# Two more pairs of gate columns through the seven-product blocks, and a new share of filler between them and the attention stages

## The chip, the cores and the metric

The kernel runs on one core of a Trainium2 chip. The metric is the device time of one launch, in microseconds (us); lower is better. Engines are called as in the profile: PE (TensorE's matmuls), PEld (its weight loads), DVE (VectorE), ACT (ScalarE), POOL (GpSimd) and SP (SyncE, which issues nearly all DMAs here).

## The reference

One layer of an encoder on 1024 tokens of width 1024, in float32. One input projection is cut into ten parts, two attentions use them, and gates mix their outputs:

```python
h = rmsnorm(x, attn_norm_g)
proj = h @ w_in
(c_q, c_kv, k_rope, z_mla, q_dil, k_dil, v_dil, z_dil,
 g_mla, g_dil) = jnp.split(proj, split_points, axis=-1)
a_out = mla_attention(c_q, c_kv, k_rope, positions, mla_q_norm_g, mla_kv_norm_g, w_uq, w_ukv)
y_mla = (a_out * jax.nn.silu(z_mla)) @ w_o_mla
d_out = dilated_mixture(q_dil, k_dil, v_dil, positions)
y_dil = (d_out * jax.nn.silu(z_dil)) @ w_o_dil
gate_mla = jax.nn.sigmoid(g_mla + b_gate[:D_MODEL])
gate_dil = jax.nn.sigmoid(g_dil + b_gate[D_MODEL:])
merged = gate_mla * y_mla + gate_dil * y_dil
return x + merged @ w_out
```

The dilated mixture has three groups of eight heads, with windows and dilations (128, 1), (512, 4), (2048, 16); their outputs are combined by softmax denominators. The latent attention has eight heads and is dense. A last RMSNorm follows. The gates' 2048 columns of `w_in` are what the change moves about.

## The kernel before, in words

**Precision.** Every float32 operand is split into a high and a low part (`split`, L148: a cast on ACT, L150, and a subtraction on POOL or DVE, L151), and a product is three matmuls (`mm3`, L142 to L146). A *column tile* is 128 columns of `w_in`; there are 48 of them in the array `wt`.

**Stages.** First come the projections (to 226.9 us in the profile): latents, rotary tables, the token factors `rcol` (one over the RMS of each token, by column) and `R` (the same as a row over all partitions), the up-projections of the latent attention, and the values of the dilated heads (`dil_v`, L422). There the order of instructions is left to a scheduler. From the block stage on the order is that of the code.

`token_factors` (L268) squares and sums the tokens, takes the inverse root on DVE (`rsqrt`, L198), copies it to `rcol` (L277), transposes it on PE (L279), copies the row (L281), and sends it through DRAM to `R`. `latents` (L338) scales the latents on DVE by `rcol` and by their own factors (L349 to L357) and transposes them on PE (L364). `dil_v` makes eight tiles of 128 tokens for each of six quarters; a tile `dv_st` takes the high part on ACT (L445), the low part on DVE (L446), and is stored by SP. There are three buffers of it.

**Block stage** (`blocks`, L649; 226.9 to 531.7 us). An item is two column tiles against all tokens, a 2 x 2 by 2 x 2 block product made with seven products in place of eight. Each is four `mm3` of 512 tokens (`block_product`, L507): 84 matmuls for an item, where plain column tiles take 96. POOL makes the differences of weight blocks (`block_minus`, L495) and splits (`block_operand`) five products ahead (`LEAD`). DVE and ACT add the products and finish: rotary embedding for twelve items of queries and keys, and for gate items the factor `R` and a tanh (the sigmoid by half angles), stored to `s_gt`. The rotary tables `cs_d` are multiplied by `R` ahead of it, in four operations on POOL (L1635). `BLOCK_GATES` (L50) names the first tile of each gate item: four items, eight of the sixteen gate tiles.

**Dilated stage** (`attention`, L1316; 531.7 to 829.7 us). The heads go in four pairs. A pair has two heads each of the groups 0 and 1, four units a head, and two units of group 2 ("class units"): 18 units a pair, 72 in all. A *tick* t works on several units at once, in this order (L1332 to L1352):

```python
do(t, 3)        # transposes: PE, then a cast on ACT (L1152)
do(t + 2, 0)    # scores: PE (L1120, L1121)
do(t, 4)        # low part: DVE (L1156)
do(t + 2, 1)    # masked maxima: DVE (L1130)
self.feed(DIL_FEED[g])
do(t - 2, 6)    # copy of half a result: ACT (L1180), every other tick
do(t + 2, 2)    # exponentials: ACT (L1137)
do(t - 2, 7)    # sum of a result: DVE (L1194), every other tick
self.feed(DIL_FEED[g])
do(t - 1, 5)    # values: PE (L1168, L1175)
```

Class units have their own lines (scores L1231, exponential L1242, transposes L1248, cast L1250, values L1262). When a unit is the last of a head, the load of the queries and keys of the head after the next is issued (`at_r<-s_dq`, `at_r<-s_dk`). The combine of a pair (`combine`, L1371) runs under the next pair's ticks: statistics through DRAM, exponents, quotients, factors through DRAM (`s_rr`), and products on POOL and DVE (L1450, sums L1454).

**Filler.** `feed(n)` (L66) adds n to a debt and issues that many steps of `gate_fill` (L718). This makes plain column tiles, `ZG` (L49): the eight tiles of z and the other eight gate tiles. A tile has 16 steps, a step one `mm3` of 512 tokens. Around its matmuls a tile needs a weight load of 512 KB, two casts on ACT and two subtractions on POOL, and for each half a product with `R` on DVE (L728), a tanh on ACT (L730 for z, L734 for gates), for z two operations on POOL (L731, L732), and a store. `DIL_FEED` (L32) has the steps of each of the two feeds in a tick: by group 0, 1, 2, and 3 for the ticks behind the last unit. Nine steps go ahead of the first tick. What is left is spread over the first 29 ticks of the latent attention (829.7 to about 1146 us), behind which come the output projections.

Of the kernel before, what the change touches and what calls it, by code (L numbers as in the profile page):

```python
# [10 lines left out]
F32 = mybir.dt.float32  # L11
# [19 lines left out]
FIRST_FEED = 9  # L31
DIL_FEED = (1.33, 1.33, 2.3, 1.8)  # L32

# [14 lines left out]

ZG = (4, 5, 6, 7, 0, 1, 2, 3, *range(16, 24))  # L49
BLOCK_GATES = (8, 10, 12, 14)  # L50

# [9 lines left out]
class Net:  # L61
# [205 lines left out]

    def token_factors(self, xp, pp):  # L268

        nc, a = self.nc, self.a  # L270
        ss = xp.tile([128, 8], F32, name="x_ss", bufs=1)
        for t in range(8):
            x = xp.tile([128, D], F32, name="x_in")
            self.dma(x, a["x"][128 * t:128 * t + 128, :])
            nc.scalar.activation(out=x, in_=x, func=AF.Square, accum_out=ss[:, t:t + 1])
        y = self.rsqrt(ss, 1.0 / D, xp, 8)
        nc.vector.tensor_copy(self.rcol, y)  # L277
        pt = pp.tile([128, 512], F32, name="pj")
        nc.tensor.transpose(pt[:8, :128], y, self.ident)  # L279
        row = xp.tile([8, 128], F32, name="x_row", bufs=1)  # L280
        nc.vector.tensor_copy(row, pt[:8, :128])  # L281
        self.dma(self.rs, row)
        flat = self.rs.rearrange("a b -> (a b)")
        self.dma(self.R, flat.partition_broadcast(128))
# [137 lines left out]
    def dil_v(self, g, quad, tp, pj):  # L422
# [12 lines left out]
        for t in range(8):  # L435
# [7 lines left out]
            if g < 2:  # L443
                st = tp.tile([128, 4, 2, 64], F32R, name="dv_st")
                nc.scalar.mul(st[:, :, 0], pv, f)  # L445
                nc.vector.scalar_tensor_tensor(out=st[:, :, 1], in0=pv, scalar=f, in1=st[:, :, 0].bitcast(F32), op0=ALU.mult, op1=ALU.subtract)  # L446
                x = slice(quad * 512, quad * 512 + 512)
                if g == 0:
                    dst = self.dv[0][128 * t + 64:128 * t + 192, x]
                else:  # L450

                    dst = self.dv[1].rearrange("(r m) x -> m r x", r=4)[32 * t:32 * t + 32, :, x]
                self.dma(dst, st.rearrange("p h a d -> p (h a d)"))
            else:
                st = tp.tile([128, 4, 64], F32, name="dv_s2")
                nc.scalar.mul(st, pv, f)
                self.dma(self.dv[2][2 * quad:2 * quad + 2, 128 * t:128 * t + 128].rearrange("a t x -> t a x"), st.rearrange("p (a h) d -> p a (h d)", h=2))
# [191 lines left out]
    def blocks(self, items, tp, pp):  # L649
# [14 lines left out]
        with self.tc.manual_schedule():  # L664
            for x in range(1, places + 14):
# [15 lines left out]
                self.block_minus(j + LEAD + 1, items)  # L681

                if x == places - 1:
                    self.close_sums()
                    self.open_areas(0)
                    for load in self.items[0][:2]:
                        load()
# [883 lines left out]
    def run(self):  # L1571
        tc, nc = self.tc, self.nc
        with ExitStack() as ctx:
# [28 lines left out]
            with tc.tile_pool(name="wpx", reuse_waits="tile", bufs=2, side="right") as self.wpx, tc.tile_pool(name="cosd", reuse_waits="tile", bufs=1, side="right") as dpool, ExitStack() as sums:  # L1602
                with tc.tile_pool(name="pj_a", reuse_waits="tile", bufs=NB_A, space=PSUM) as pj, tc.tile_pool(name="dvp", reuse_waits="tile", bufs=3, side="right") as vp:
                    with tc.tile_pool(name="lp", reuse_waits="tile", bufs=1) as lp, tc.tile_pool(name="pj_l", reuse_waits="tile", bufs=8 - NB_A, space=PSUM) as pl:
                        with tc.tile_pool(name="wl", reuse_waits="tile", bufs=1) as wl, tc.tile_pool(name="xp", reuse_waits="tile", bufs=3) as xp:
                            self.latent_proj(lp, wl, xp, pj)
                            self.tables(xp)
                            self.token_factors(xp, pl)
                            m = cp.tile([128, 896], F32, name="masks")
# [17 lines left out]
                    with tc.tile_pool(name="bs", reuse_waits="tile", bufs=1) as tp:  # L1627
                        self.block_sums(sp, tp)
                        self.dil_v(1, 0, vp, pj)
                    for g, quad in ((1, 1), (2, 0), (2, 1)):  # L1630
                        self.dil_v(g, quad, vp, pj)
                    for x in (self.cos_d, self.sin_d):
                        for half in range(2):
                            c = slice(512 * half, 512 * half + 512)
                            nc.gpsimd.tensor_tensor(out=x[:, c], in0=x[:, c], in1=self.R[:, c], op=ALU.mult)  # L1635
                    for r in (0, S + 64):
# [106 lines left out]
```

## Time and profile before

| | |
|---|---|
| three runs | 1252.14, 1256.76, 1256.94 us; median 1256.76 |
| the profiled execution | 1254.46 us |
| its span | 1252.5 us, mean granted clock of PE 0.99 |
| PE busy | 1212.4 us (97%), 6909 matmuls |
| PEld, DVE, ACT, POOL busy | 1064.5, 730.8, 622.0, 570.2 us |
| DMA | 221.37 MB, 177 GB/s in the mean |

The profile is of one execution. A line of the timeline has the start from the beginning of the span, the length, the engine, the line of the kernel, the operation, its output and inputs with their shapes; in brackets stands how long the engine was idle just before, and who ended that. A line of groups has, behind the bar, the busy time, the mean length in ns, and the idle time before these instructions. A matmul is listed with its whole latency, so matmuls overlap and the distance of their starts tells the pace. A wait costs time only on the engine that the rest waits for.

### The profile page before, as it was taken

To read this page: it belongs to the slowest core of one execution; us is meant where nothing else is said; L and a number is where in the kernel's file an instruction comes from. 1 tells how busy PE (TensorE), PEld (TensorE's weight loads), DVE (VectorE), ACT (ScalarE), POOL (GpSimd) and SP (SyncE) were. 2 spreads that over 40 slices of the span, in tenths; PEclk is the share of its full clock that TensorE was granted. 3 is DMA by queue.
4 is the path that set the end of the run, shared out by engine and by line. 5 is a ranking of instruction groups with operands and counts; after the bars stand their busy time and mean duration, and the time that the engine had idled before them with its cause. 6 is when DMAs were issued, how large, how long until landed. Compare 5 with 4: busy or idle time off the path is not lost.

```text
span 1252.5 us, 19486 instructions
## 1 busy us (share of the span) xinstructions
PE 1212.4 (97%) x6909; PEld 1064.5 (85%) x6909; DVE 730.8 (58%) x1304; ACT 622.0 (50%) x1300; POOL 570.2 (46%) x482
## 2 busy tenths in 40 slices
PE   8979999999999999999999999999999999999998
PEld 8979999888888888888888889878878888888886
DVE  7473534467657653345555575647766767759542
ACT  6534345444343344455554666545655656654232
POOL 2352218877777777543464442415521201168322
PEclk9989999999999999999999999899999999999999
DMA  9847589365445642496887898964634445225241
GB/s 333 225 157 283 196 302 317 103 180 156 135 132 165 174 127 100 122 268 197 233 257 200 207 294 212 266 175 116 178 128 119 110 118 135 85 96 182 84 151 51
DMA packets 126416, 221.37 MB, mean 177 GB/s; under 512 B 28072, under 2 KB 60400, under 8 KB 121392
## 3 DMA queue, kind: packets, MB, share of 16 engines
q1 hardware_dynamic: 126320, 220.14, 59.5%
q8 instruction: 54, 0.88, 0.3%
q14 instruction: 42, 0.34, 0.1%
HBM read 149.24 MB, written 70.85 MB: 176 GB/s over the span
## 4 chain that ended last, share of the span: by engine, by line
PE 75%; DMA 11%; DVE 4%; ACT 4%; issue 3%; POOL 1%; SPq 1%; ACTq 0%; POOLq 0%; DVEq 0%
PE bank L145 5%; PE bank L144 5%; PE bank L146 5%; PE pj L145 4%; PE bank L871 4%; PE pj L144 4%; PE pj L146 4%; DMA at_r<-s_dk 3%; PE st_a L144 2%; PE st_a L145 2%; PE st_d L145 2%; PE st_c L145 2%; PE st_d L146 2%; PE st_a L146 2%; PE st_c L146 2%
## 5 line engine op out<-in xcount | busy, mean ns | idle before, releaser
L151 POOL TENSOR_TENSOR w_l<-w_raw,w_h 128x512 fp32r<-128x512 f32 x188 | 247.5, 1330 | 276.7 <-ACT w_h L150 218.1
L150 ACT CAST w_h<-w_raw 128x512 fp32r<-128x512 f32 x188 | 112.6, 621 | 110.1 <-POOL w_raw L495 92.7
L144 PE MATMUL bank<-at_r,w_h 128*128 128x512 f32 x344 | 142.8, 415 | 0.0
L879 DVE TENSOR_TENSOR at_r<-bank,at_r 128x512 fp32r<-128x512 f32 x128 | 88.0, 688 | 84.5 <-ACT at_r L873 84.2
L145 PE MATMUL bank<-at_r,w_h 128*128 128x512 f32 x344 | 136.6, 397 | 0.6 <-POOL at_r L151 0.6
L146 PE MATMUL bank<-at_r,w_l 128*128 128x512 f32 x344 | 136.7, 397 | 0.0
L873 ACT CAST at_r<-bank 128x512 fp32r<-128x512 f32 x128 | 74.9, 586 | 72.5 <-PE bank L871 71.9
L145 PE MATMUL pj<-w_l,at_r 128*128 128x256 f32 x384 | 109.7, 286 | 0.0
L146 PE MATMUL pj<-w_h,at_r 128*128 128x256 f32 x384 | 109.6, 285 | 0.0
L144 PE MATMUL pj<-w_h,at_r 128*128 128x256 f32 x384 | 109.5, 285 | 0.0
L1137 ACT ACTIVATE at_f<-at_f,at_f 128x256 f32<-128x256 f32 x128 | 64.1, 502 | 52.1 <-DVE at_f L1130 51.8
L1156 DVE TENSOR_TENSOR at_r<-bank,at_r 128x512 fp32r<-128x512 f32 x64 | 43.9, 686 | 70.4 <-ACT at_r L1152 70.3
L495 POOL TENSOR_TENSOR w_raw<-w_raw 128x512 f32<-128x512 f32 x64 | 82.8, 1294 | 0.1
L871 PE MATMUL bank<-consts,at_f 128*128 128x128 f32 x512 | 77.2, 273 | 1.7 <-ACT at_f L863 1.1
L146 PEld LDWEIGHTS bank<-at_r,w_l 128*128 128x128 f32 x344 | 65.7, 191 | 14.9
L146 PEld LDWEIGHTS pj<-w_h,at_r 128*128 128x128 f32 x384 | 74.2, 193 | 1.0
L145 PEld LDWEIGHTS pj<-w_l,at_r 128*128 128x128 f32 x384 | 74.3, 193 | 0.7
L144 PEld LDWEIGHTS pj<-w_h,at_r 128*128 128x128 f32 x384 | 74.2, 193 | 0.7
L145 PEld LDWEIGHTS bank<-at_r,w_h 128*128 128x128 f32 x344 | 65.9, 192 | 9.9 <-POOL at_r L151 1.0
L144 PEld LDWEIGHTS bank<-at_r,w_h 128*128 128x128 f32 x344 | 65.8, 191 | 9.2
L895 PE MATMUL bank<-at_r,at_r 128*128 128x256 f32 x256 | 67.7, 285 | 1.3 <-ACT at_r L873 1.3
L896 PE MATMUL bank<-at_r,at_r 128*128 128x256 f32 x256 | 67.5, 285 | 0.9 <-DVE at_r L879 0.9
(321 smaller groups left out, 3325.3 us busy)
## 6 DMA issues: line engine op xcount, KB each, us to landing
w_raw<-wt SPq DMA_DIRECT2D x48, 512.0 KB, 3.7
at_r<-s_dq SPq DMA_DIRECT2D x32, 512.0 KB, 7.3
s_dk<-dq_st SPq DMA_DIRECT2D x80, 128.0 KB, 2.4
s_dv<-dv_st SPq DMA_DIRECT2D x32, 256.0 KB, 3.0
s_dq<-dq_st SPq DMA_DIRECT2D x64, 128.0 KB, 2.4
zt<-s_gt SPq DMA_DIRECT2D x32, 256.0 KB, 4.5
w_raw<-wv SPq DMA_DIRECT2D x12, 512.0 KB, 5.8
at_r<-s_dk SPq DMA_DIRECT2D x8, 576.0 KB, 11.3
```

The source lines that it names most:

```text
L144: mm(out, lh, rh, start=start, stop=False, skip_group_check=skip)
L145: mm(out, lh, rl, start=False, stop=False, skip_group_check=skip)
L146: return mm(out, ll, rh, start=False, stop=stop, skip_group_check=skip)
L150: self.nc.scalar.copy(out=h, in_=raw)
L151: sub.tensor_tensor(out=l, in0=raw, in1=h.bitcast(F32), op=ALU.subtract)
L495: self.nc.gpsimd.tensor_tensor(out=b[out], in0=b[x], in1=b[y], op=ALU.subtract)
L871: self.nc.tensor.transpose(pt[:, o:o + 128], self.P[k, b][:, 128 * kc:128 * kc + 128], self.ident)
L873: self.nc.scalar.copy(out=h, in_=pt)
L879: self.nc.vector.tensor_tensor(out=l, in0=pt, in1=h.bitcast(F32), op=ALU.subtract)
L895: mm(out, vv[:, kc], ph[:, x], start=kc == 0, stop=False)
L896: mm(out, vv[:, kc], pl[:, x], start=False, stop=kc == 7)
L1137: nc.scalar.activation(out=p, in_=p, func=AF.Exp, scale=-1.0, bias=nm, accum_out=den)
```

## The change

Four gate tiles, 8 to 11 of the sixteen, go from the filler to the blocks as two items more (18 in place of 16), and `ZG` has 12 tiles in place of 16. The feeds of head ticks go from 1.33 to 0.77 steps, those of class ticks from 2.3 to 3.0, those behind the last unit from 1.8 to 1.4. With that 164.2 steps are issued before the latent attention, against 228.5; 27.8 and 27.5 are left for it. `dv_st` has five buffers. The transpose of the token row and its way to `R` become `token_row`, called behind the block sums. The four products of the rotary tables move from ahead of the block stage into it, behind its second to fifth product.

```diff
-DIL_FEED = (1.33, 1.33, 2.3, 1.8)
+DIL_FEED = (0.77, 0.77, 3.0, 1.4)
...
-ZG = (4, 5, 6, 7, 0, 1, 2, 3, *range(16, 24))
-BLOCK_GATES = (8, 10, 12, 14)
+ZG = (4, 5, 6, 7, 0, 1, 2, 3, *range(20, 24))
+BLOCK_GATES = (8, 10, 12, 14, 16, 18)
...
-    def token_factors(self, xp, pp):
+    def token_factors(self, xp):
...
         y = self.rsqrt(ss, 1.0 / D, xp, 8)
         nc.vector.tensor_copy(self.rcol, y)
+
+    def token_row(self, tp, pp):
+
+        nc = self.nc
         pt = pp.tile([128, 512], F32, name="pj")
-        nc.tensor.transpose(pt[:8, :128], y, self.ident)
-        row = xp.tile([8, 128], F32, name="x_row", bufs=1)
+        nc.tensor.transpose(pt[:8, :128], self.rcol, self.ident)
+        row = tp.tile([8, 128], F32, name="x_row", bufs=1)
...
-                st = tp.tile([128, 4, 2, 64], F32R, name="dv_st")
+                st = tp.tile([128, 4, 2, 64], F32R, name="dv_st", bufs=5)
...
+                if x in (2, 3, 4, 5):
+                    y, c = (self.cos_d, self.sin_d)[x // 2 - 1], slice(512 * (x % 2), 512 * (x % 2) + 512)
+                    self.nc.gpsimd.tensor_tensor(out=y[:, c], in0=y[:, c], in1=self.R[:, c], op=ALU.mult)
...
-                            self.token_factors(xp, pl)
+                            self.token_factors(xp)
...
+                    self.token_row(vp, pj)
                     for g, quad in ((1, 1), (2, 0), (2, 1)):
                         self.dil_v(g, quad, vp, pj)
-                    for x in (self.cos_d, self.sin_d):
-                        for half in range(2):
-                            c = slice(512 * half, 512 * half + 512)
-                            nc.gpsimd.tensor_tensor(out=x[:, c], in0=x[:, c], in1=self.R[:, c], op=ALU.mult)
```

How it moves instructions is seen in three places of the built programs. The first is ScalarE in the first ticks of the dilated stage. Before, from its first tick on: a cast of transposes (L1152), two exponentials (L1137), and between them a tanh of the filler (L730), the casts of its next weights (L150), or the copy of a result (L1180):

```order
L1152 CAST at_2432_r<-bank_5438 128x512
L1137 ACTIVATE at_512_f,at_96_f<-at_512_f,at_96_f 128x256 x2
L1152 CAST at_2432_r<-bank_5439 128x512
L730 ACTIVATE zt<-zt 128x512
L1137 ACTIVATE at_512_f,at_96_f<-at_512_f,at_96_f 128x256 x2
L1152 CAST at_2432_r<-bank_5438 128x512
L1137 ACTIVATE at_512_f,at_96_f<-at_512_f,at_96_f 128x256 x2
L150 CAST w_h<-w_raw 128x512 x2
L1152 CAST at_2432_r<-bank_5439 128x512
```

The same lines of the changed kernel are L1159, L1144, L737 and L1187. This is its fourth to sixth tick; the three ticks ahead of them hold nothing but casts and exponentials:

```order
L1159 CAST at_2432_r<-bank_5743 128x512
L1187 COPY at_512_f<-left_5749 64x512
L1144 ACTIVATE at_512_f,at_96_f<-at_512_f,at_96_f 128x256 x2
L737 ACTIVATE zt<-zt 128x512
L1159 CAST at_2432_r<-bank_5742 128x512
L1144 ACTIVATE at_512_f,at_96_f<-at_512_f,at_96_f 128x256 x2
L1159 CAST at_2432_r<-bank_5743 128x512
L1187 COPY at_512_f<-left_5750 64x512
L1144 ACTIVATE at_512_f,at_96_f<-at_512_f,at_96_f 128x256 x2
L150 CAST w_h<-w_raw 128x512 x2
L1159 CAST at_2432_r<-bank_5742 128x512
```

The order of a tick's own work is the same; a tile's filler is spread over some ten ticks where it was over six, and in these the tanh now stands behind the exponentials, where it stood ahead of them.

The second place is VectorE in the projections, at the value tiles (`dv_st`) and the factors of the latents (`lat_sc`, `rs_y`). Before, the fourth value tile stands ahead of the steps of the inverse root (L207 to L209), and all sixteen scalings of the latents behind them:

```order
L446 SCALAR_TENSOR_TENSOR dv_st<-pj,rcol,dv_st 128x4x64 x2
L281 COPY x_row<-pj 8x128
L446 SCALAR_TENSOR_TENSOR dv_st<-pj,rcol,dv_st 128x4x64
L349 SCALAR_TENSOR_TENSOR lat_sc<-lat_ss,rcol 128x4 x4
L350 TENSOR_TENSOR lat_sc<-lat_sc,rcol 128x4 x4
L203 TENSOR_SCALAR lat_sc<-lat_sc 128x8 x2
L204 TENSOR_SCALAR rs_i<-lat_sc 128x8 x2
L205 TENSOR_SCALAR rs_y<-rs_i 128x8 x2
L446 SCALAR_TENSOR_TENSOR dv_st<-pj,rcol,dv_st 128x4x64
L207 TENSOR_TENSOR rs_u<-rs_y 128x8 x2
```

In the changed kernel the last steps of the inverse root, the eight scalings of the first half of the latents (L361), and only then the fourth value tile (L450):

```order
L209 SCALAR_TENSOR_TENSOR rs_y<-rs_u,rs_y 128x8
L361 TENSOR_SCALAR lat<-lat,rs_y 128x256 x2
L361 TENSOR_SCALAR lat<-lat,rs_y 128x128 x2
L361 TENSOR_SCALAR lat<-lat,rs_y 128x256
L361 TENSOR_SCALAR lat<-lat,rs_y 128x128
L361 TENSOR_SCALAR lat<-lat,rs_y 128x256
L361 TENSOR_SCALAR lat<-lat,rs_y 128x128
L357 TENSOR_TENSOR rs_y<-rs_y,rcol 128x4 x2
L450 SCALAR_TENSOR_TENSOR dv_st<-pj,rcol,dv_st 128x4x64
```

On PE the latents' first transposes are instruction 317 of the program's matmuls, where they were the 344th; the token row's transpose (the 256th before) is gone from there. On ScalarE both splits of the query weights (`uq_h`) now stand ahead of the latents' high parts (`lat_h`), where the second stood behind the first two of them.

The third place is POOL. Before, the four products of the rotary tables stood in the projections, ahead of the split of the query weights:

```order
L151 TENSOR_TENSOR w_l<-w_raw,w_h 128x512 x8
L1635 TENSOR_TENSOR cs_d<-cs_d,at_1024_f 128x512 x4
L151 TENSOR_TENSOR uq_l<-u_raw,uq_h 128x768
L151 TENSOR_TENSOR w_l<-w_raw,w_h 128x512 x3
L151 TENSOR_TENSOR uq_l<-u_raw,uq_h 128x768
```

Now they stand one by one (L689) between the operands of the first item of the block stage:

```order
L151 TENSOR_TENSOR w_l<-w_raw,w_h 128x512
L689 TENSOR_TENSOR cs_d<-cs_d,at_1024_f 128x512
L151 TENSOR_TENSOR w_l<-w_raw,w_h 128x512
L689 TENSOR_TENSOR cs_d<-cs_d,at_1024_f 128x512
L151 TENSOR_TENSOR w_l<-w_raw,w_h 128x512
L499 TENSOR_TENSOR w_raw<-w_raw 128x512
L689 TENSOR_TENSOR cs_d<-cs_d,at_1024_f 128x512
L151 TENSOR_TENSOR w_l<-w_raw,w_h 128x512
L499 TENSOR_TENSOR w_raw<-w_raw 128x512
L689 TENSOR_TENSOR cs_d<-cs_d,at_1024_f 128x512
```

The splits of the query weights no longer stand behind these products on POOL; the products stand behind the second to fifth product of the block stage.

## What the change will do: the prediction

> **What bounds the kernel now.** I first cut the span in the table by windows: block products from 226.9 to 531.7, dilated attention to 829.7; then the four runs of head units inside the dilated stage (from a pair's first transposes to those of its first class unit, 16 ticks each). Columns: length, then busy time of PE, PEld, DVE, ACT and POOL, granted clock, DMA share, GB/s.
>
> ```profile
> 226.90:531.70 304.80, 304.80 (x1345) 252.46 (x1346) 170.92 (x272) 127.09 (x241) 218.70 (x179) 1.00 0.50 140
> 531.70:829.70 298.00, 287.87 (x1768) 254.72 (x1766) 172.19 (x438) 165.92 (x430) 126.16 (x126) 0.98 0.86 236
> 542.20:597.20 55.00, 54.66 (x348) 48.80 (x347) 28.90 (x85) 33.61 (x91) 26.38 (x24) 1.00 0.77 218
> 609.70:668.00 58.30, 57.04 (x366) 50.71 (x366) 37.13 (x96) 35.50 (x93) 36.49 (x37) 1.00 0.85 229
> 681.90:740.50 58.60, 57.83 (x369) 51.38 (x369) 36.26 (x95) 34.47 (x91) 28.41 (x30) 1.00 0.82 215
> 753.50:815.90 62.40, 60.58 (x369) 53.94 (x368) 40.64 (x98) 36.23 (x93) 20.88 (x24) 0.95 0.88 234
> ```
>
> The block stage is TensorE alone: 304.8 us busy of 304.8 for 16 items, 19.05 us an item. The dilated stage looks nearly as full, so the timeline has to show what sets its ticks. Two matmuls of the block stage stand first, for the pace; then TensorE, ScalarE and VectorE in head ticks of the dilated stage.
>
> ```profile
> 526.22 0.39 PE L144 MATMUL st_c<-s_h,w_h 128*128 128x512 f32 x1
> ...
> 528.94 0.39 PE L144 MATMUL st_d<-at_r,w_h 128*128 128x512 f32 x1
> ```
> ```profile
> 584.37 0.64 PE L1175 MATMUL left<-at_r,at_r 128*128 128x256 f32 x4
> 584.85 0.60 PE L1144 MATMUL bank<-consts,at_f 128*128 128x128 f32 x4
> ...
> 585.76 0.39 PE L144 MATMUL bank<-at_r,w_h 128*128 128x512 f32 x1
> ```
> ```profile
> 574.97 0.58 ACT L1152 CAST at_r<-bank 128x512 fp32r<-128x512 f32 x1
> ...
> 576.70 0.51 ACT L1137 ACTIVATE at_f<-at_f,at_f 128x256 f32<-128x256 f32 x1 [0.55 <-DVE at_f L1130]
> ...
> 577.82 0.59 ACT L1152 CAST at_r<-bank 128x512 fp32r<-128x512 f32 x1
> ...
> 584.75 0.58 ACT L1152 CAST at_r<-bank 128x512 fp32r<-128x512 f32 x1
> ...
> 587.44 0.57 ACT L1152 CAST at_r<-bank 128x512 fp32r<-128x512 f32 x1
> ```
> ```profile
> 575.57 0.69 DVE L1156 TENSOR_TENSOR at_r<-bank,at_r 128x512 fp32r<-128x512 f32 x1 [2.39 <-ACT at_r L1152]
> 576.18 0.42 DVE L1130 CUSTOM_DVE_ANT_0 at_f<-right,masks 128x256 f32<-128x256 f32 x1
> ```
>
> Twelve block matmuls start within 2.72 us, 0.227 us each, so a filler step (three of them) is 0.68 us of TensorE. A head tick of group 1 without filler costs TensorE 585.76 - 584.37 = 1.39 us (values, transposes, scores). With 2 x 1.33 steps it costs 1.39 + 1.81 = 3.20 us, close to the 3.4 to 3.9 us that a tick takes (55.0 to 62.4 over 16).
>
> But there is a second ring, nearly as long. The cast at 574.97 on ScalarE lets VectorE start the low part at 575.57; behind it, in VectorE's order, come the masked maxima (576.18); on the first of them waits the first exponential (576.70); and behind the two exponentials, in ScalarE's order, stands the next cast (577.82). That is 2.85 us. The tick at 584.75, without a copy of results, takes 2.69. Neither holds any filler. In the mean **2.77 us is the least that a head tick can take**, whatever TensorE has to do in it.
>
> **The change, part by part**, in the program's order.
>
> *Value tiles and the token row.* The projection stage holds one long chain of waits, through four engines:
>
> ```profile
> 63.71 1.10 ACT L445 ACTIVATE dv_st<-pj,rcol 128x256 fp32r<-128x256 f32 x2 [8.11 <-DMA s_dv<-dv_st]
> 64.22 0.48 DVE L446 SCALAR_TENSOR_TENSOR dv_st<-pj,rcol,dv_st 128x256 fp32r<-128x256 f32 x1 [6.23 <-ACT dv_st L445]
> 66.21 4.96 POOL L1635 TENSOR_TENSOR cs_d<-cs_d,at_f 128x512 f32<-128x512 f32 x4 [19.52 <-DVE rs_u L208]
> 67.45 2.52 DVE L353 TENSOR_TENSOR rs_y<-rs_y,rcol 128x4 f32<-128x4 f32 x4
> 53.86 0.27 PE L279 MATMUL pj<-consts,rs_y 128*8 128x128 f32 x1 [1.89 <-DVE rs_y L209]
> 71.38 0.69 PE L364 MATMUL pj<-consts,lat 128*128 128x128 f32 x2 [6.81 <-DVE lat L357]
> ```
>
> ScalarE's fourth value tile waits 8.11 us for a store to free a buffer, VectorE behind it 6.23, with the latents' factors queued there, and TensorE 6.81 for those. With five buffers that store is not waited for. The token row's transpose leaves this place, and its 1.89 us with it. VectorE's small operations (2.52 us for four of them while POOL multiplies the tables) lose their neighbour. What is late next: in the new order TensorE comes to the latents 27 instructions earlier, before the factors can be done, so I leave it a wait of 3 us. That is 8.7 - 3, about **-6 us**. Ends: -10 if nothing else is late; -2 if the query weights, which ScalarE must now split ahead of the latents, come late. The token row itself is needed only at the blocks, 100 us later: 0.
>
> *Blocks.* Two more items: 2 x 19.05 = **+38.1 us**. VectorE (171 of 304.8 us), ScalarE (127) and POOL (219) have room for them. Their weight loads and gate stores leave SP's queue in the dilated stage (DMA share 0.86) for this one (0.50): 0. The rotary products cost POOL 4 x 1.24 us (4.96 above) between the operands of the first item; POOL prepares those five products ahead, 5 x 2.72 us, so 0. Without that cover they would cost up to 5 us.
>
> *Filler taken from head ticks.* If TensorE set every tick, 2 x (1.33 - 0.77) steps, 0.76 us, would leave each of 64 head ticks, 48.8 us in all. But TensorE's need falls to 1.39 + 1.05 = 2.44 us, below the ring, and the saving stops there. By the new order on ScalarE, the first pair's 14 ordinary ticks hold on the ring one tanh and one pair of casts behind the exponentials (a second tanh stands where ScalarE waits anyway): 0.63 + 2 x 0.62 = 1.9 us.
>
> ```profile
> L150 ACT CAST w_h<-w_raw 128x512 fp32r<-128x512 f32 x188 | 112.6, 621 | 110.1 <-POOL w_raw L495 92.7 <-POOL at_r L151 5.1 <-DMA w_raw<-wom 3.7
> L730 ACT ACTIVATE zt<-zt 128x512 f32<-128x512 f32 x16 | 10.1, 629 | 22.7 <-DVE zt L728 16.5 <-DMA s_zs<-zt 6.2
> L1231 PE MATMUL right<-at_f,at_f 128*128 128x64 f32 x128 | 16.1, 282 | 0.0
> ```
>
> A pair's last two head ticks hold a class unit's scores, 16.1 / 8 = 2.0 us, in place of a head's 0.5: now 3.20 + 1.5 = 4.7, then 3.9 us on TensorE. So the first pair takes 14 x 2.77 + 1.9 + 7.8 = 48.5, against 55.0. Under the other three runs lies the combine of the pair before, whose waits stand inside the ring:
>
> ```profile
> 649.24 1.49 DVE L1450 TENSOR_TENSOR at_f<-at_f 128x512 f32<-128x512 f32 x2 [2.67 <-DMA at_f<-s_rr]
> ...
> 653.15 1.09 DVE L1194 TENSOR_TENSOR at_f<-left,at_f 64x512 f32<-64x512 f32 x1 [1.14 <-POOL at_f L1454]
> ...
> 658.94 0.97 DVE L1450 TENSOR_TENSOR at_f<-at_f,at_f 128x512 f32<-128x512 f32 x1 [0.60 <-DMA at_f<-s_rr]
> ```
>
> These 4.4 us come from latencies, not from filler, so I keep them. For the combine's four products on VectorE and the TensorE-bound tick that opens a run I add 3.2 (an estimate: 1.5 us of products that find no gap, and 4.5 us in place of 2.77 for a tick with a class unit's sixteen value products, as with its scores). That makes 56.1 a run, against 58.3, 58.6 and 62.4. Over the four: 6.5 + 2.2 + 2.5 + 6.3 = **-17.5 us**. Ends: -33 without such waits; -4 if the shorter ticks uncover as much again.
>
> *Class ticks.* Eight ticks get 2 x (3.0 - 2.3) steps more, 0.95 us each: **+7.6**. The wait that opens them stands ahead of a tick's filler, so more filler doesn't hide it:
>
> ```profile
> L1120 PE MATMUL right<-at_r,at_r 128*128 128x256 f32 x128 | 38.3, 322 | 5.9 <-DMA at_r<-s_dk 5.9
> ```
>
> The keys are asked for three ticks ahead. Those ticks lose some 2 us, the load doesn't, though fewer weight loads stand before it on SP: **+2** over three pairs (0 to 7). *Edges:* two ticks ahead of the first lose 1.5 us, two behind the last, with 4 x (1.8 - 1.4) steps less, 1.1: **-2.6**.
>
> *The clock.* It fell twice in the dilated stage, in the last run above (0.95) and here:
>
> ```profile
> 660.00:680.00 20.00, 18.08 (x104) 15.73 (x103) 11.92 (x27) 9.54 (x24) 9.10 (x8) 0.91 0.95 258
> ```
>
> At half rate, 0.91 over 20 us is 1.8 us lost, and 0.95 over 62.4 is 3.1. I carry both over. The Trainium skill ("TensorE: Matmul & The Clock Gate", HAM oscillation) sets the border at idle gaps of about 3.4 us; by it the clock would stay up here, and the sum would be 5 us lower. The trace does not agree: in this window TensorE is idle for 2 us in all.
>
> **The sum**, on the profiled execution's 1254.46 us (2.3 below the median of the runs, which I don't add): -6 + 38.1 - 17.5 + 7.6 + 2 - 2.6 = +21.6, so **1276 us**. Its own range is 1262 to 1291, since the ends of the terms seldom meet.
>
> **The rivals.** *TensorE sets the ticks after all* (ends faster). Then all 64.3 steps that leave the stage count, 64.3 x 0.68 = 43.7 us, against 38.1, with 6 early: 1254.5 - 11.7 = **1243**. It decides if head ticks can run at 2.5 us. For it: PE busy 288 of 298. Against it: the two ticks without filler, 2.69 and 2.85. Chance 0.12. The Trainium skill ("Perfetto Trace Analysis", Identifying the Most-Contended Engine) judges TensorE's headroom by its weight loads; with 255 us of 298 here and 252 of 305 in the blocks it would favour this rival. The trace speaks against that measure: the blocks have no slack at the lower share.
>
> *The ring holds, but its waits vanish*, as POOL and SP carry less filler: 13.2 less in three runs, nothing for the keys, 10 early: 1276 - 19, about **1257**, no change. For it: one DMA and one POOL operation are at fault. Against: they follow on each other, and shorter ticks leave them less time. 0.12.
>
> *The clock drops more often*, as each tick now holds idle TensorE time: five more drops at 1.8 to 3.1 us, +13, **1289**. For it: the two drops. Against: three of four runs show 1.00. 0.10. *The moves don't do what they say*: the order shows that they do; no chance given.
>
> **How the numbers follow.** The forecast has 0.66. About 0.5%, 6.3 us around the median of 1256.76, is what a measurement of this kernel can tell: faster is below 1250.5, slower above 1263. The first rival and a little more make faster 0.13; the second and the forecast's lower edge make the same 0.15; the rest, slower, 0.72. A range from 1250 to 1291 leaves out the first rival and half of the third.
>
> **What would show it.** Right: a block stage of some 343 us; casts of head ticks 2.7 to 3.0 us apart, and TensorE's transposes waiting for exponentials in most ticks; runs of 48 to 57 us; class ticks about 1 us longer; TensorE's early wait down from 6.81 to about 3. Wrong: runs near 45 us, casts nearer than 2.6 us, or no waits for the combine.

## The result and the profile after

The changed kernel takes 1285.06 us in the median of four runs (1278.60 to 1285.99), beside 1256.38 us of the kernel before in its runs: ratio 1.0246, 95% interval 1.0212 to 1.0281. It is slower, by some 29 us. The profiled execution took 1284.35 us, its span 1282.4. I cut it at the same places of the program as before: block stage, dilated stage, the latent attention, and the four runs of head ticks (columns as in the first table of the prediction).

```profile
0.00:227.50 227.50, 211.59 (x1497) 204.20 (x1498) 114.90 (x225) 112.35 (x225) 84.23 (x65) 0.98 0.75 254
227.50:570.20 342.70, 342.70 (x1514) 283.78 (x1513) 180.81 (x288) 142.76 (x267) 249.87 (x205) 1.00 0.48 136
570.20:857.90 287.70, 262.91 (x1585) 225.50 (x1584) 165.65 (x431) 156.56 (x415) 115.17 (x118) 0.95 0.85 230
857.90:1156.00 298.10, 288.70 (x1743) 252.98 (x1743) 201.35 (x262) 177.52 (x322) 83.34 (x73) 0.99 0.45 121
579.40:627.20 47.80, 44.43 (x293) 38.33 (x292) 28.38 (x84) 31.93 (x89) 16.91 (x17) 1.00 0.82 225
645.90:702.00 56.10, 51.39 (x314) 43.96 (x314) 36.92 (x96) 33.48 (x90) 27.87 (x30) 0.94 0.85 229
714.60:771.50 56.90, 51.64 (x315) 44.32 (x314) 37.04 (x95) 32.32 (x88) 27.66 (x30) 0.91 0.88 223
783.90:837.90 54.00, 49.00 (x311) 41.94 (x311) 33.83 (x92) 31.17 (x86) 21.57 (x25) 0.97 0.86 216
```

| us, from the first matmul of each stage | before | after | difference | forecast |
|---|---|---|---|---|
| projections | 226.9 | 227.5 | +0.6 | -6 |
| blocks | 304.8 | 342.7 | +37.9 | +38.1 |
| dilated stage | 298.0 | 287.6 | -10.4 | -10.5 |
| of it the four head runs | 55.0, 58.3, 58.5, 62.4 | 47.8, 56.1, 56.9, 54.0 | -19.4 | -17.5 |
| of it the ticks ahead of the first run | 10.5 | 9.2 | -1.3 | -1.5 |
| of it the class ticks and the end | 12.5, 13.9, 13.0, 13.8 | 18.7, 12.5, 12.4, 20.0 | +10.4 | +8.5 |
| latent attention | 296.4 | 298.1 | +1.7 | 0 |
| output | 126.4 | 126.4 | 0 | 0 |

In the dilated stage the busy time of TensorE falls by 25 us, and the stage by 10: for the rest, some 15 us, TensorE is idle. Four views show why. First a head tick without a copy of results, in the first run (the lines of the ring alone):

```profile
600.31 0.59 ACT L1159 CAST at_r<-bank 128x512 fp32r<-128x512 f32 x1
600.93 0.69 DVE L1163 TENSOR_TENSOR at_r<-bank,at_r 128x512 fp32r<-128x512 f32 x1 [1.92 <-ACT at_r L1159]
601.54 0.41 DVE L1137 CUSTOM_DVE_ANT_0 at_f<-right,masks 128x256 f32<-128x256 f32 x1
602.06 0.51 ACT L1144 ACTIVATE at_f<-at_f,at_f 128x256 f32<-128x256 f32 x1 [1.16 <-DVE at_f L1137]
602.71 0.33 PE L1151 MATMUL bank<-consts,at_f 128*128 128x128 f32 x1 [1.04 <-ACT at_f L1144]
603.05 0.56 ACT L1159 CAST at_r<-bank 128x512 fp32r<-128x512 f32 x1
```

Cast, low part, maxima, exponential, next cast: 2.74 us, the ring of the prediction. TensorE's transposes (602.71) now wait for the exponential at the end of it. Then the groups of waits in the dilated stage, of TensorE for exponentials and keys, and of VectorE for the combine's factors. First before, then after:

```profile
L1144 PE MATMUL bank<-consts,at_f 128*128 128x128 f32 x256 | 39.8, 275 | 1.9 <-ACT at_f L1137 1.7
L1450 DVE TENSOR_TENSOR at_f<-at_f 128x512 f32<-128x512 f32 x6 | 6.3, 1082 | 2.7 <-DMA at_f<-s_rr 2.7
L1450 DVE TENSOR_TENSOR at_f<-at_f,at_f 128x512 f32<-128x512 f32 x6 | 5.3, 883 | 2.2 <-DMA at_f<-s_rr 2.2
```
```profile
L1151 PE MATMUL bank<-consts,at_f 128*128 128x128 f32 x256 | 46.4, 289 | 10.9 <-ACT at_f L1144 10.4
L1127 PE MATMUL right<-at_r,at_r 128*128 128x256 f32 x128 | 38.7, 325 | 5.2 <-issue 3.9 <-DMA at_r<-s_dk 1.3
L1457 DVE TENSOR_TENSOR at_f<-at_f 128x512 f32<-128x512 f32 x6 | 5.7, 991 | 3.4 <-DMA at_f<-s_rr 3.4
L1457 DVE TENSOR_TENSOR at_f<-at_f,at_f 128x512 f32<-128x512 f32 x6 | 4.1, 680 | 9.6 <-DMA at_f<-s_rr 9.6
```

TensorE's wait for exponentials rises from 1.7 to 10.4 us, VectorE's for the factors from 4.9 to 13.0. The two largest single ones are 3.88 us in the first combine and 4.15 in the third. Behind the first, in VectorE's order, stands the low part, on which TensorE's values wait:

```profile
691.98 0.69 DVE L1457 TENSOR_TENSOR at_f<-at_f,at_f 128x512 f32<-128x512 f32 x1 [3.88 <-DMA at_f<-s_rr]
692.59 0.68 DVE L1163 TENSOR_TENSOR at_r<-bank,at_r 128x512 fp32r<-128x512 f32 x1
693.33 0.62 PE L1182 MATMUL left<-at_r,at_r 128*128 128x256 f32 x3 [1.24 <-DVE at_r L1163]
```

Then the clock, here behind that wait (columns as in the first table, the granted clock third from the end; windows of 1, 6 and 1 us):

```profile
694.00:695.00 1.00, 0.53 (x2) 0.35 (x3) 0.96 (x1) 0.98 (x5) 1.00 (x2) 0.93 1.09 246
695.00:701.00 6.00, 6.00 (x24) 5.53 (x24) 4.35 (x7) 2.42 (x5) 3.32 (x4) 0.50 0.99 259
701.00:702.00 1.00, 1.00 (x6) 0.89 (x5) 0.97 (x2) 0.25 (x1) 0.00 (x0) 0.66 1.16 445
```

The dilated stage holds four such phases at half rate (from 630.0, 694.9, 756.3 and 831.4, in all 27 us) where it held two (10 us). Last the end of the stage, where a gate tile's product on VectorE waits 10.40 us for a store, and TensorE 2.53 for VectorE:

```profile
852.54 0.69 DVE L735 TENSOR_TENSOR zt<-bank,at_f 128x512 f32<-128x512 f32 x1 [10.40 <-DMA s_gt<-zt]
853.37 0.47 PE L144 MATMUL bank<-at_r,w_h 128*128 128x512 f32 x1 [2.53 <-DVE zt L735]
```

### The profile page after: what moved, and what is told of

Its sections match the earlier page's. It is cut to its first block, busy times and chain, and to the rows that moved or that the text cites. A ratio compares the mean times of both kernels' runs of the same rounds, so it can differ in the third digit from the quotient of the medians.

```text
span 1282.4 us, 19478 instructions
## 1 busy us (share of the span) xinstructions
PE 1226.1 (96%) x6885; PEld 1066.8 (83%) x6885; DVE 729.9 (57%) x1314; ACT 627.8 (49%) x1312; POOL 584.8 (46%) x496
## 5 line engine op out<-in xcount | busy, mean ns | idle before, releaser
L151 POOL TENSOR_TENSOR w_l<-w_raw,w_h 128x512 fp32r<-128x512 f32 x194 | 254.7, 1325 | 261.2 <-ACT w_h L150 214.0
L150 ACT CAST w_h<-w_raw 128x512 fp32r<-128x512 f32 x194 | 116.4, 621 | 122.0 <-POOL w_raw L499 104.6
L144 PE MATMUL bank<-at_r,w_h 128*128 128x512 f32 x284 | 120.8, 425 | 4.0 <-DVE zt L735 4.0
L145 PE MATMUL bank<-at_r,w_h 128*128 128x512 f32 x284 | 113.9, 401 | 0.5 <-POOL at_r L151 0.5
L146 PE MATMUL bank<-at_r,w_l 128*128 128x512 f32 x284 | 114.1, 402 | 0.0
L1144 ACT ACTIVATE at_f<-at_f,at_f 128x256 f32<-128x256 f32 x128 | 64.1, 502 | 75.6 <-DVE at_f L1137 75.5
L499 POOL TENSOR_TENSOR w_raw<-w_raw 128x512 f32<-128x512 f32 x72 | 93.2, 1294 | 0.0
L146 PEld LDWEIGHTS bank<-at_r,w_l 128*128 128x128 f32 x284 | 54.9, 193 | 12.7
L144 PEld LDWEIGHTS bank<-at_r,w_h 128*128 128x128 f32 x284 | 55.4, 195 | 11.5 <-issue 2.9
L878 PEld LDWEIGHTS bank<-consts,at_f 128*128 128x128 f32 x512 | 59.8, 141 | 3.6 <-ACT at_f L870 2.2
```

Source lines behind the costliest of these rows:

```text
L144: mm(out, lh, rh, start=start, stop=False, skip_group_check=skip)
L145: mm(out, lh, rl, start=False, stop=False, skip_group_check=skip)
L146: return mm(out, ll, rh, start=False, stop=stop, skip_group_check=skip)
L150: self.nc.scalar.copy(out=h, in_=raw)
L151: sub.tensor_tensor(out=l, in0=raw, in1=h.bitcast(F32), op=ALU.subtract)
L499: self.nc.gpsimd.tensor_tensor(out=b[out], in0=b[x], in1=b[y], op=ALU.subtract)
```

## The experiments

The theory: short head ticks are held by the ring of ScalarE and VectorE, and beside it by transfers that come late. The rivals: TensorE with its clock holds them; or transfers alone do. "The gates" are the two items more in the blocks with their filler and feeds; "the early edits" are the five value buffers, the later token row and the rotary products in the blocks. For these the question is whether their gain is there, or given back behind them. Times are medians; the ratio is to runs of the kernel before on the same chip, with its 95% interval, and so the better measure of a gain.

The last two columns are of one profiled execution each, and that can lie beside the median: e5_halfq's was 6.7 us below it, e11_early_halfq's 5.4 below, e2_swap's 4.8 and e13_early_raw2's 4.6 above.

| run | us | ratio | dilated stage, us | first head run, us |
|---|---|---|---|---|
| the changed kernel | 1285.06 | 1.0246 (1.0212 to 1.0281) | 287.6 | 47.8 |
| e1_early | 1252.0 | 0.9988 (0.9960 to 1.0016) | 295.7 | 54.7 |
| e10_gates | 1279.02 | 1.0201 (1.0170 to 1.0231) | 283.6 | 47.9 |
| e2_swap | 1274.73 | 1.0158 (1.0119 to 1.0197) | 280.0 | 43.1 |
| e3_late | 1287.2 | 1.0272 (1.0241 to 1.0303) | 290.9 | 47.5 |
| e4_nofill | 1359.19 | one run | 274.8 | 46.5 |
| e5_halfq | 1273.95 | 1.0183 (1.0144 to 1.0223) | 274.1 | 47.3 |
| e6_swap_halfq | 1263.65 | 1.0093 (1.0060 to 1.0127) | 266.4 | 42.4 |
| e8_early_swap | 1255.39 | 1.0024 (1.0002 to 1.0046) | 296.0 | 54.2 |
| e11_early_halfq | 1247.2 | 0.9938 (0.9909 to 0.9967) | 287.1 | 55.0 |
| e9_five_swap | 1265.68 | 1.0110 (1.0076 to 1.0143) | 290.8 | 48.1 |
| e12_shift | 1288.12 | 1.0268 (1.0227 to 1.0308) | 292.9 | 51.4 |
| e13_early_raw2 | 1247.74 | 0.9939 (0.9918 to 0.9960) | 300.6 | 54.9 |

**The ring alone: no filler in head ticks.**

```diff
-DIL_FEED = (0.77, 0.77, 3.0, 1.4)
+DIL_FEED = (0.0, 0.0, 3.0, 1.4)
```

> The changed kernel with no filler in head ticks; the 99 steps that they held go to the latent attention, so only the dilated stage is compared. Ring theory: the first run of 16 head ticks takes 44 to 47 us (16 x 2.77 and a little), against 47.8 with filler, casts 2.7 to 2.9 us apart; total 1335 to 1350. Rival (TensorE sets the ticks): at 1.45 us of its own work a tick and 3 us for the class units' scores, 26 to 32 us for that run; total 1270 to 1300.

With filler that late some z tiles are read (from 846.0 us on) before the last is stored (939.9), so the output is another one. The first run of head ticks took 46.5 us, inside the ring's 44 to 47 and far from the 26 to 32 of the rival; its fourteen ordinary ticks have their casts 2.76 us apart in the mean. Here is that run, 16 ticks:

```profile
573.10:619.60 46.50, 35.51 (x220) 29.49 (x220) 26.23 (x83) 28.75 (x86) 5.22 (x7) 0.89 0.80 214
```

TensorE is idle or at half rate for much of it, and still the run is only 1.3 us shorter than with 0.77 steps a feed. The three runs with a combine under them took 50.3 to 50.9 us, so the ring alone doesn't hold those. The total was missed (1359 against 1335 to 1350). Behind the dilated stage the kernel is 93 us longer than the changed one, where some 100 filler steps of 0.68 us would be 68; what the other 25 are isn't settled.

**The ring opened: maxima ahead of the low part.**

```diff
             do(t + 2, 0)
-            do(t, 4)
             do(t + 2, 1)
+            do(t, 4)
```

> The changed kernel with the masked maxima ahead of the low part in VectorE's order. Ring theory: an exponential then no longer waits behind a cast and its low part, the ring of 2.7 to 2.85 us is open, head ticks fall to what TensorE needs, about 2.45 us in the mean; 48 ordinary head ticks gain some 0.3 us each, total down by 10 to 18 us, to 1268 to 1275. Rival (ticks are held by TensorE with its lower clock and by the combine's transfers): no change within 3 us, 1282 to 1288; runs of 48 to 57 us stay.

1274.73 us, 10.3 less, and the intervals of the two ratios don't meet. A maximum waits for scores now, the exponential for nothing, and the cast for TensorE:

```profile
596.96 0.42 DVE L1137 CUSTOM_DVE_ANT_0 at_f<-right,masks 128x256 f32<-128x256 f32 x1 [0.54 <-PE right L1128]
597.23 0.59 ACT L1159 CAST at_r<-bank 128x512 fp32r<-128x512 f32 x1
597.71 0.51 ACT L1144 ACTIVATE at_f<-at_f,at_f 128x256 f32<-128x256 f32 x1
597.85 0.69 DVE L1163 TENSOR_TENSOR at_r<-bank,at_r 128x512 fp32r<-128x512 f32 x1
599.28 0.59 ACT L1159 CAST at_r<-bank 128x512 fp32r<-128x512 f32 x1 [0.48 <-PE bank L1151]
```

In the first run the casts are 2.37 us apart in the mean (2.87 in the changed kernel), the run is 43.1 us, and TensorE is busy for 42.4 of them. So the ring was the limit there. In the second and third runs the gain is small (55.6 and 55.1 us, from 56.1 and 56.9): something else holds them.

**The late transfers: products two ticks later.**

```diff
-LAST_STEPS = {3: 4, 4: 6, 5: 8, 6: 9, 8: 14, 9: 15, 10: 17, 11: 19, 12: 20}
+LAST_STEPS = {3: 4, 4: 6, 5: 8, 6: 9, 8: 14, 9: 15, 10: 17, 13: 19, 14: 20}
...
-                8: lambda: (weighted(1, 0, p), weighted(1, 1, p)), 9: step9, 10: step10, 11: step11, 12: step12}
+                8: lambda: (weighted(1, 0, p), weighted(1, 1, p)), 9: step9, 10: step10, 13: step11, 14: step12}
```

> The changed kernel with the last products and sums of the combine two ticks later (13 and 14 in place of 11 and 12). Theory of transfers uncovered by shorter ticks: the wait of VectorE for the second spread of the quotients (3.9 us in the first combine, 9.6 in all three) is gone, and with it part of the clock drops beside it; total down by 8 to 15 us, to 1270 to 1277. Rival (the ring is what holds those ticks, the wait only shifts where the time shows): within 3 us of the changed kernel, 1282 to 1288.

No gain, 1287.2 us. But the rival's reason is wrong too: VectorE's waits for the factors fell from 13.0 to 3.1 us and the second run from 56.1 to 49.4, and the class ticks behind that run rose from 12.5 to 21.6. The time came back as a wait for keys:

```profile
670.00:700.00 30.00, 21.48 (x138) 18.30 (x138) 19.23 (x46) 16.49 (x42) 17.70 (x15) 0.94 1.01 269
```
```profile
699.24 0.55 PE L1127 MATMUL right<-at_r,at_r 128*128 128x256 f32 x1 [7.23 <-DMA at_r<-s_dk]
```

For the 30 us ahead of it the DMA engines are busy all the time (share 1.01). Ticks that come sooner there meet loads that come no sooner.

**Fewer bytes: half query loads, alone, with the swap, and with the gates of before.**

```diff
-            for rows in (slice(0, 64), slice(64, 128)):
+            for rows in (slice(0, 64), slice(64, 128))[:2 if g == 0 and (hh or not pair) else 1]:
```

> The changed kernel without the second half of the query load (rows 64 to 127, 512 KB) for 11 of the 16 heads of the dilated stage; these heads then use stale rows, so the values of the dilated attention are changed and only the time counts. Theory of full transfers (in the second half of each pair the DMA engines are busy 100% of the time, and that, not the ring, holds the pairs 2 to 4 at 67 to 69 us): some 6 us of transfers leave each pair, the waits for keys and for the combine shrink, dilated stage down from 287.6 to 268 to 277, total 1268 to 1277. Ring theory (transfers only add the waits at the class ticks): the first run stays at 47 to 48 us, only the waits at the class ticks go, dilated stage 281 to 288, total 1279 to 1287.

> Both: the masked maxima ahead of the low part, and 11 half query loads left out (values changed as there). If ring and transfers each hold a part of the ticks, the gains add up: dilated stage 260 to 270 (280.0 with the swap alone), total 1255 to 1266. If transfers alone held pairs 2 to 4, the same as with half the queries alone within 4 us. If TensorE and its clock set what is left, 276 to 281.

> The control of the half query loads: the same 11 loads left out (values changed as there), with the early edits but with the gates, filler and feeds of before. If transfers hold the short ticks of the changed kernel and TensorE those of before: -2 to -5 us against before, ratio 0.996 to 0.998 (0.9988 without it). If transfers held both kernels alike: -9 to -13, ratio 0.990 to 0.993.

Alone it gives 11.1 us (1273.95), with the swap 21.4 (1263.65; the swap alone 10.3). By the ratios, which leave out the difference of chips, it is 0.6% alone, 1.5% with the swap and 0.9% for the swap alone, of the time before. Either way the gains add up, so ring and transfers each hold a part; that of the transfers is the less certain, as the interval without the halves (1.0144 to 1.0223) still meets the changed kernel's. As issues and their landing times show (size of one, then the median time to landing), keys and factors come sooner; first the changed kernel, then without the halves:

```profile
at_r<-s_dk SPq DMA_DIRECT2D x8, 512.0 KB, 10.6
at_f<-s_rr SPq DMA_DIRECT2D x12, 128.0 KB, 7.3
```
```profile
at_r<-s_dk SPq DMA_DIRECT2D x8, 512.0 KB, 7.2
at_f<-s_rr SPq DMA_DIRECT2D x12, 128.0 KB, 5.4
```

The total and the stage (274.1 us) are those of full transfers; the first run stayed at 47.3 us, as the ring has it, and the runs with combines under them fell (56.1 to 51.4, 56.9 to 54.1, 54.0 to 51.4). But that profile has less of the low clock too: the stage holds 14 us at half rate in place of 27, so up to 6.8 of its 13.5 us may be the clock's. The control is between what the two theories gave: 0.9938 against 0.9988 with the whole loads (e1_early), 0.5% where the changed kernel gained 0.6%. The two intervals just meet. So late transfers seem to cost the kernel before nearly as much as the changed one; they are no price of short ticks alone.

**The swap with the gates of before.**

```diff
-            do(t, 4)
             do(t + 2, 1)
+            do(t, 4)
```

> The early edits with the gates, filler and feeds of before (1252.0 us, 0.9988 of before), and the maxima ahead of the low part. Here TensorE has 3.2 us of work in a head tick, so an open ring should give little: ring theory 0 to -4 us, ratio to before 0.995 to 0.999. Rival (the swap shortens something else that every tick pays, as the 10 us that it gave in the changed kernel): -8 to -12 us, ratio 0.990 to 0.992.

1.0024, no gain, if anything a loss, and a little above the 0.995 to 0.999 expected. With 3.2 us of TensorE in a tick the ring isn't the limit, so opening it gives nothing; the rival's 8 to 12 us are excluded.

**Halfway: five gate items, with the swap.**

```diff
-DIL_FEED = (0.77, 0.77, 3.0, 1.4)
+DIL_FEED = (1.05, 1.05, 2.65, 1.6)
...
-ZG = (4, 5, 6, 7, 0, 1, 2, 3, *range(20, 24))
-BLOCK_GATES = (8, 10, 12, 14, 16, 18)
+ZG = (4, 5, 6, 7, 0, 1, 2, 3, *range(18, 24))
+BLOCK_GATES = (8, 10, 12, 14, 16)
```

> Five gate items in the blocks in place of six (filler tiles 14, feeds 1.05, 1.05, 2.65, 1.6, halfway between the two kernels), with the maxima ahead of the low part. If TensorE sets the ticks once the ring is open: blocks 323.7, dilated stage 276 to 280, total 1253 to 1258, as fast as before. If transfers hold the pairs: dilated stage 283 to 288, total 1261 to 1267.

1265.68 us, inside the range of the transfers, and not TensorE's 1253 to 1258. The dilated stage, 290.8, is above both ranges: it lost only some 7 us against 298.0, with 30 steps less, and the blocks grew by 20. So TensorE alone isn't the limit, and the transfers don't account for the whole size.

**Filler moved within the runs.**

```diff
-DIL_FEED = (0.77, 0.77, 3.0, 1.4)
+DIL_FEED = (0.4, 1.14, 3.0, 1.4)
```

> The changed kernel with filler moved inside the runs of head ticks, from the first eight (feeds 0.4 in place of 0.77) to the last eight (1.14), where the waits for the combine and most low clocks are. If those waits are idle time that filler can fill: total down by 5 to 10 us, 1274 to 1279. If the ring holds the first eight and the transfers, to which this adds, the last eight: 0 to +6, 1284 to 1291.

1288.12 us, 3 more in the median, and its ratio lies inside the changed kernel's interval. Idle time behind late transfers could not be filled this way: VectorE's waits for factors fell from 13.0 to 2.3 us, as in the kernel with later products, and TensorE's waits ahead of scores rose from 5.2 to 12.3, 9.3 of them for keys.

**The early edits, alone and left out.**

```diff
-DIL_FEED = (0.77, 0.77, 3.0, 1.4)
+DIL_FEED = (1.33, 1.33, 2.3, 1.8)
...
-ZG = (4, 5, 6, 7, 0, 1, 2, 3, *range(20, 24))
-BLOCK_GATES = (8, 10, 12, 14, 16, 18)
+ZG = (4, 5, 6, 7, 0, 1, 2, 3, *range(16, 24))
+BLOCK_GATES = (8, 10, 12, 14)
```

The second kernel is the opposite: the three lines of the change that this one takes back, and nothing else.

> The kernel before with the three early edits alone (five value buffers, the token row later, the rotary products in the blocks); gates, filler and feeds as before. Theory (what the latents gain is given back behind them, at the block sums): projections end within 2 us of 226.9 us, and the total is within 3 us of the kernel before, 1253 to 1260. Rival (the early edits are worth their 6 us, and what cancelled them in the changed kernel is chance): projections end at 219 to 222, total 1247 to 1251.

> The kernel before with the gates, filler and feeds of the change alone, without the early edits. Early edits worth nothing: ratio to before 1.022 to 1.028, blocks 342.7, dilated stage 285 to 291. Rival (the early edits gave some 6 us that other waits hide): ratio 1.029 to 1.033.

Alone they give 0.9988, no difference that can be told from none; 6 us would be 0.9952, just outside the interval. The 1252.0 us lie between the ranges of theory and rival, and the projections (to 227.9 us) are the theory's. Without the early edits, the gates and feeds give 1.0201, a little under what I expected and under the 1.0246 with them, though the intervals overlap. So no gain of them shows, and the forecast's -6 us is refuted. Two things are behind it. The wait that they remove is not the same in every execution: in e10, whose projections are those of the kernel before, the same buffer wait was 7.12 us where it had been 8.11, but TensorE's wait for the latents' factors was 1.56 where it had been 6.81 (2.29 more came behind it, for the latents' low part):

```profile
61.27 0.47 ACT L445 ACTIVATE dv_st<-pj,rcol 128x256 fp32r<-128x256 f32 x1 [7.12 <-DMA s_dv<-dv_st]
64.68 0.44 PE L364 MATMUL pj<-consts,lat 128*128 128x128 f32 x2 [1.56 <-DVE lat L357]
```

And in the changed kernel another wait stands in its place, of the latents' high parts for the query weights ahead of them on ScalarE:

```profile
62.63 1.85 POOL L151 TENSOR_TENSOR uq_l<-u_raw,uq_h 128x768 fp32r<-128x768 f32 x1 [16.44 <-ACT uq_h L150]
64.51 0.33 SPq L140 DMA_DIRECT2D u_raw<-wuq  x1
68.16 0.83 ACT L150 CAST uq_h<-u_raw 128x768 fp32r<-128x768 f32 x1 [4.87 <-DMA u_raw<-wuq]
68.90 1.26 ACT L371 ACTIVATE lat_h<-pj,consts 128x512 fp32r<-128x512 f32 x2
70.42 0.90 PE L368 MATMUL pj<-consts,lat 128*128 128x128 f32 x3 [4.85 <-DVE lat_l L372]
217.53 0.58 PE L144 MATMUL pj<-w_h,at_r 128*128 128x256 f32 x1 [2.95 <-ACT dv_s L460]
```

The raw query weights have one buffer; the second half is asked for at 64.51, when POOL has read the first, and lands at 68.16. TensorE then waits 4.85 us, and at the end of the stage 2.95 more, for a copy of values that stands behind a cast of the block sums on ScalarE. Over the profiles of eleven kernels with these same early instructions the stage ended between 222.4 and 228.8 us, in the mean at 226.0; the two kernels without the edits ended it at 226.9 and 223.9. The spread is as wide as the term itself.

**A second buffer for the query weights.**

```diff
-            raw = lp.tile([128, 1024], F32, name="u_raw")
+            raw = lp.tile([128, 1024], F32, name="u_raw", bufs=2)
```

> The early edits with the gates, filler and feeds of before (0.9988 of before), and two buffers for the raw query weights, so that the second half is loaded without waiting for the split of the first. If that load is what gave the early gain back: the latents' high parts on ScalarE come some 4 us earlier, TensorE's wait for the latents' low part falls from about 5 us to under 2, ratio to before 0.993 to 0.997. If the value stores and weight loads before it keep the transfers full (the first half itself took 11 us to land), or the block sums behind it take the gain: 0.997 to 1.001.

With the early edits and the gates of before: 1247.74 us, 0.9939 (0.9918 to 0.9960). It is 0.6% faster than the kernel before; its interval just meets that of the early edits alone (0.9960 to 1.0016), so the buffer's own share is likely, not shown. The profile denies the way I had for it. TensorE's wait at the latents is as long as it was, since ScalarE now splits the third raw tile, of the other up-projection, ahead of the high parts:

```profile
68.72 1.04 ACT L150 CAST ukv_h<-u_raw 128x1024 fp32r<-128x1024 f32 x1 [4.54 <-DMA u_raw<-wukv]
69.68 1.26 ACT L371 ACTIVATE lat_h<-pj,consts 128x512 fp32r<-128x512 f32 x2
71.20 1.12 PE L368 MATMUL pj<-consts,lat 128*128 128x128 f32 x4 [4.90 <-DVE lat_l L372]
```

The stage ended at 221.5 us all the same, the earliest of all though by less than a microsecond, with no wait of TensorE over half a microsecond behind this one. Whether the smaller waits behind it went because the query weights were ready or because the order behind them changed isn't settled.

## Why the prediction was right, and where not

Slower was forecast, at 1276 us in a range of 1250 to 1291, and 1285 measured. The sum was +21.6 us; against the profiled execution it is +29.9.

- **Blocks, +38.1:** +37.9. Eighteen items at 342.7 / 18 = 19.04 us, and TensorE was busy for all of it, so the rotary products on POOL were covered.
- **Head ticks, -17.5:** -19.4. The ring was right, by the ticks without filler (2.76 us) and by opening it (-10.3 us). The first run came to 47.8 us against 48.5, the others to 56.1, 56.9 and 54.0 against 56.1. That these three came so near is in part luck. I read 4.4 us of waits off the first combine and charged them to all three; VectorE's waits for factors were 4.9 us in all before and 13.0 after. The reason was only half right too: I took those waits for fixed latencies, and they move with the load of the DMA engines (the factors landed after 7.3 us in the median, with fewer bytes after 5.4), which are full in the second half of a pair (share 1.03 from 749 to 770 us). And the fourth run's 62.4 us held 3.1 of low clock which its 56.1 left out, though I said that both drops were carried over; with them the sum would have been 1279.
- **Class ticks, keys and edges, +7.6 + 2 - 2.6:** +9.1. The size is near, its parts are not. The edge behind the last unit was misread: the fourth feed applies to the second of those two ticks alone, and this stands behind the first matmul of the latent attention. The first takes the class feed. So 18 filler steps, not 12, stand between the last class ticks' first transposes and the end of the stage (13 before), and this tick cost 0.95 us more where I took off 0.5. The stage lost 61 steps and not 64. There TensorE also waited 2.53 us behind the store of a gate tile (at 853.37, above). The first pair's class ticks grew by 6.2 us, with 3.87 us ahead of the next head's scores and the clock at half rate behind it. The view calls these 3.87 "issue", but the load of those keys, asked for at 619.65, landed at 631.58, and the scores began at 631.67. The waits at the second and third vanished, since late factors ahead of them gave the keys time: when e3_late took that wait away, the keys were waited for again.
- **Value tiles and the token row, -6:** this step failed, and makes 6.6 of the 8.3 us by which the forecast was short. I took TensorE's 6.81 us of one execution for the price of the buffers. In another execution of the same instructions it was 1.56, and the query weights, which I had named as the lower end (-2), took its place, with 4.85 us where I had left 3.
- **The clock, carried over:** wrong by five phases of 3.4 us in the dilated stage, 27 us at half rate in place of 10, so up to 8.5 us. Since part of that time TensorE would have waited, it isn't all loss. One phase more in the latent attention fits that stage's +1.7 us.

Of the rivals, "TensorE sets the ticks after all" fell with the ticks without filler, and the one whose waits vanish fell with the 13.0 us for factors. "The clock drops more often" came true in part: there are two drops more and not five, but most of them are longer. Its 1289 is nearer to the measured time than the forecast; yet the terms above put most of what the forecast lacked into the projections, and not into the dilated stage.

The Trainium skill ("TensorE: Matmul & The Clock Gate", HAM oscillation) would have kept the clock up for want of an idle gap of 3.4 us. The drop from 694.9 us speaks against that border here: in the 3.4 us ahead of it the longest idle time of TensorE was the 1.24 us ahead of 693.33, and it was busy for half of them; ahead of the drop from 831.4 the longest was 0.96 us, and TensorE was busy for 2.44 of 3.4. First the window ahead of 694.9:

```profile
691.50:694.90 3.40, 1.64 (x9) 0.88 (x8) 2.92 (x7) 1.23 (x5) 2.15 (x2) 0.99 1.03 231
```

The same page of the Trainium skill (A second HAM failure mode) tells of frequent small idles between groups of matmuls, there from cycling through PSUM banks, that make the clock oscillate. The idle times here are of that kind; what exactly makes the clock fall, no run here isolates.

## What to carry to other kernels

Before work is taken out of a stage, look for the loop through the other engines that would hold it next, and read it off ticks that happen to hold no such work: the two here gave it as 2.77 us, and without filler it measured 2.76. When a loop like this holds, the order of two instructions on one engine can be worth more than the work: in the first run the swap gave 4.7 us, and leaving out all filler 1.3. A result needed a tick later stood ahead of one needed at once. And a wait for a transfer in one execution is a sample, not a price: look what stands behind it in the same queue, and whether the gain is larger than the spread of the stage.

## What the runs showed of the hardware

- The clock of TensorE falls to 0.50 for phases of 3.4, 6.8 or 10.2 us, in the run without filler also of 13.7 and 20.5: always a multiple of 3.4, but for the phase that the end of an execution cuts short. The dilated stage had two before (3.4 and 6.8 us) and four after (6.8, 6.8, 10.2, 3.4). The step agrees with the activity window of some 3.4 us in the Trainium skill ("TensorE: Matmul & The Clock Gate", Part 1: The HAM clock gate). Each 3.4 us at half rate cost up to 1.7 us.
- With the DMA engines busy for 0.85 of the dilated stage, the same key load took 10.6 us in the median to land, and 7.2 us with 9% fewer bytes in the stage (60.15 MB beside 66.00) and a share of 0.79.
